# Two fused transformer blocks: all low parts of the weights made by VectorE, none by GpSimd

## The chip, the cores and the metric

The kernel runs on one core of a Trainium2 chip. Five engines work side by side, each through its own instructions in their written order: TensorE (PE in the rows: matmuls and transposes; PEld is its weight load), VectorE (DVE), ScalarE (ACT), GpSimd (POOL) and SyncE (SP), which here starts the loads of the weights. An engine waits at a semaphore when an operand or a buffer is not ready, and all that stands behind that instruction in its queue waits too. The metric is device time in microseconds of one execution, lower is better; several runs give a median.

## The reference

Two blocks follow each other on 256 tokens of width 1024, all in fp32.

```python
# first block: layer 0 MoBA, layer 1 forgetting attention (FoX), both 16 heads of 64
for layer in range(2):
    hn = rms_norm(h, attn_norm[layer])
    ...
    h = h + merge_heads(mix) @ w_o[layer]
    h = h + squared_relu_mlp(rms_norm(h, mlp_norm[layer]), w_up[layer], w_down[layer])
return rms_norm(h, final_norm)

# second block: modulated by c through w_ada
h = modulate(rmsnorm(x, norm_ffn1), sh1, sc1)
x = x + 0.5 * g1 * swiglu(h, ffn1_w_gate, ffn1_w_up, ffn1_w_down)
h = modulate(rmsnorm(x, norm_mix), sh2, sc2)
x = x + g2 * hybrid_mixer(h, ...)          # SSD scan and MLA attention side by side
h = modulate(rmsnorm(x, norm_ffn2), sh3, sc3)
x = x + 0.5 * g3 * swiglu(h, ffn2_w_gate, ffn2_w_up, ffn2_w_down)
return rmsnorm(x, norm_final)
```

## The kernel before

The weights (240 MB) pass through the core once, as slabs of 128 partitions by 1024 fp32 numbers. SyncE loads a slab into `raw` (5 buffers). To keep fp32 precision each slab is split in two: a rounded high part `wh`, a cast by ScalarE (L174), and a low part `wl` = raw - wh, a subtraction with two inputs in SBUF (L175). Both go into tiles with 5 buffers. A product is then three matmuls: high by high, high by low, low by high (L212 to L214 where tokens are the rows of the result, L245 to L247 where features are). The activations are split in the same way by `split`: cast L259 on ScalarE, subtraction L260 on VectorE. Slabs that carry a gain take the lines L178 and L179 instead and always have both halves on ScalarE and VectorE.

The low part at L175 is VectorE's work, except for 38 slabs which the set `on_pool` names: these are GpSimd's. Some first slabs of a stage are made early, before their stage begins (the `early` argument): in pieces, with the cast L167 to `qh` and the subtraction L168 to `ql`. All 18 of these `ql` are GpSimd's.

What stands where in each queue is decided by the program's order. `take(i)` hands a slab to the matmuls and prepares up to two slabs ahead of it; side jobs such as the softmax of the attention are generators which `tick()` advances by a step after each piece of matmuls. So the instructions for a future slab come to stand between instructions of the softmax, on each engine in the same relative order. TensorE's order is fixed as well: pieces of a projection, then a piece of attention, then a projection again.

The stages are named A0 (MoBA layer), M0 (its MLP), A1 (FoX layer), M1, F1 (first SwiGLU), the mixer, F2 (second SwiGLU). In A0 and A1 the attention of 8 heads goes in six halves through `half`: VectorE makes the biased scores `pr` (L620 in A0, L627 in A1) and their maximum `m` (L532); ScalarE the exponentials with their sum (L535); VectorE the reciprocal `rs` (L539), GpSimd the product of pr and rs (L540); TensorE transposes it (L545), ScalarE copies the transposed `pT` out (L547), TensorE multiplies by the values (L638), and the result is split (L259, L260). On ScalarE a slab's wh L174 often stands right behind the exponentials and the pT of an earlier half behind that.

Where one stage hands over to the next, the residual is finished and normalised before TensorE can begin: into F1 by `two_norms_chain` (VectorE's L844, L1020, L1024 on four pieces, ScalarE's square sums, GpSimd's `v` L310, L1028 and `y` L317, then VectorE's `hn` L980 and TensorE's transposes L265); into the mixer and F2 by `norm_chain` with VectorE's `gated` L988, `h` L989, `hn` L1000 in their place. In the mixer, `log1p_of` (L335 to L344, small operations on VectorE) leads to `dA` (L1148), with which TensorE goes on at L1152.

Of the kernel before, what the change touches and what calls it, by code (L numbers as in the profile page):

```python
# [13 lines left out]
OP = mybir.AluOpType  # L14
# [8 lines left out]
F2 = 2816  # L23
# [5 lines left out]
def kernel(ctx: ExitStack, tc: tile.TileContext, a: dict, out: bass.AP):  # L29
    nc = tc.nc  # L30
    PE, ACT, DVE, POOL = nc.tensor, nc.scalar, nc.vector, nc.gpsimd
# [34 lines left out]
    def tt(shape, name="t", dt=F32):  # L66
        return tiny.tile(list(shape), dt, tag="t", name=name)

    def f(ap):
        return ap.bitcast(F32)  # L70
# [43 lines left out]
    ada_order = [(None, j, half, kk) for j in range(9) for half in range(2) for kk in range(4)]  # L114
    mixed = {"rate": 0.0, "due": 0.0}
    hold = []
    on_pool = set()

    def slab(w, r0, nk, c0, n, gain=None, m=None, early=0):


        m = m or max(1, 1024 // n)
        got = []
        for k in range(0, nk, m):
            j = min(m, nk - k)
            plan.append((w, r0 + k * TP, j, c0, n, None if gain is None else gain[k:k + j], len(got) < early))
            got.append(len(plan) - 1)
            mixed["due"] += mixed["rate"]
            if mixed["due"] >= 1 and ada_order:
                mixed["due"] -= 1  # L130
                plan.append(ada_order.pop(0))
        return got
# [22 lines left out]
    def prepare():  # L155
        i = at["prep"]
        raw, e = ready.pop(i), plan[i]
        at["prep"] += 1
        if e[0] is None:
            ada_step(raw, *e[1:])  # L160
            return
        m, n, gain = e[2], e[4], e[5]
        if e[6]:
            ready[i] = []
            for k in range(m):
                hi, lo = pair("q", (TP, n))
                ACT.copy(hi, raw[:, k])  # L167
                POOL.tensor_tensor(lo, raw[:, k], f(hi), op=OP.subtract)  # L168
                ready[i].append((hi, lo))
            return  # L170
        hi = whp.tile([TP, m, n], F32R, tag="wh", name="wh")
        lo = whp.tile([TP, m, n], F32R, tag="wl", name="wl")
        if gain is None:
            ACT.copy(hi, raw)  # L174
            (POOL if i in on_pool else DVE).tensor_tensor(lo, raw, f(hi), op=OP.subtract)  # L175
        else:
            for k in range(m):
                ACT.mul(hi[:, k], raw[:, k], gain[k])  # L178
                DVE.scalar_tensor_tensor(out=lo[:, k], in0=raw[:, k], scalar=gain[k], in1=f(hi[:, k]),  # L179
                                         op0=OP.mult, op1=OP.subtract)  # L180
        ready[i] = [(hi[:, k], lo[:, k]) for k in range(m)]
        at["live"] += 1

    def take(i):

        load_ahead()
        more = 0 if hold else 2 if i else 1
        while at["prep"] < len(plan):
            e = plan[at["prep"]]
            if at["prep"] > i:  # L190
                early = e[0] is not None and e[6]
                if not more or not (early or at["live"] < WB):
                    break
                more -= e[0] is not None and not early
            prepare()
            load_ahead()
        return ready[i]
# [56 lines left out]
    def pair(tag, shape=(TP, 512)):  # L254
        return sb(tag, shape, F32R, tag + "h"), sb(tag, shape, F32R, tag + "l")
# [133 lines left out]
    def plan_attention(qkv, w_o):  # L389
        ids = {}  # L390
        for g in range(2):
            for n in ((2, 0, 1) if g == 0 else (0, 1, 2)):
                w, c0, gain = qkv[n]
                ids["qkv"[n], g] = slab(w, 0, 8, c0 + g * 512, 512, gain)
        for g in range(2):
            for s in range(2):
                ids["o", g, s] = slab(w_o, g * 512, 4, s * 512, 512)
        return ids

    def plan_hidden(ups, w_down, cuts, rate, early=0, after=0):  # L400

        up, down = [], []
        for j in range(len(cuts) + 1):
            mixed["rate"] = rate if after < j < len(cuts) - 1 else 0.0
            if j < len(cuts):
                c0, n = cuts[j]
                up.append([slab(w, 0, 8, c0, n, g, m=2 if n == 512 else 4, early=early if j + i == 0 else 0)
                           for i, (w, g) in enumerate(ups)])
            if j > 0:
                c0, n = cuts[j - 1]  # L410
                down.append([slab(w_down, c0, n // TP, s * 512, 512) for s in range(2)])
        mixed.update(rate=0.0, due=0.0)
        return up, down
# [5 lines left out]
    A0 = plan_attention([(wq, n * D, g_attn[0]) for n in range(3)], a["w_o"][0])  # L419
    M0 = plan_hidden([(a["w_up"][0], g_mlp[0])], a["w_down"][0], MLP_CUTS, 0.5, after=1)  # L420
    A1 = plan_attention([(a["fox_w_q"][0], 0, g_attn[1]), (a["w_kv"], 0, g_kv), (a["w_kv"], D, g_kv)], a["w_o"][1])
    M1 = plan_hidden([(a["w_up"][1], g_mlp[1])], a["w_down"][1], MLP_CUTS, 0.45)
    F1 = plan_hidden([(a["ffn1_w_gate_2"][0], None), (a["ffn1_w_up_2"][0], None)], a["ffn1_w_down_2"][0], FFN_CUTS,
                     0.55, 3)
    X = {"dt": slab(w_in, 0, 8, 2560, 400, early=3), "ckv": slab(w_in, 0, 8, 2960, 288, m=2),
         "bc": slab(w_in, 0, 8, D + 1024, 512)}
# [8 lines left out]
    for n, (r0, c) in enumerate(((D, 73), (D + 512, 77), (0, 65), (512, 69))):  # L435
        for s in range(2):
            X["out", n, s] = slab(w_out, r0, 4, s * 512, 512, col_list(cols2, c, 4))
    F2 = plan_hidden([(a["ffn2_w_gate_2"][0], None), (a["ffn2_w_up_2"][0], None)], a["ffn2_w_down_2"][0], FFN_CUTS,
                     0.3, 3)
# [36 lines left out]
    def ada_step(raw, j, half, kk):  # L476
        n = 2 * j + half
        if kk == 0:
            if half == 0:
                ada[j] = dram.tile([1, D], F32, name=f"mod{j}")  # L480
            ada["acc"] = ada.pop("next", None) or ada_begin(n)
        acc = ada["acc"]
        for i in range(2):
            k = 2 * kk + i
            DVE.scalar_tensor_tensor(out=acc, in0=raw[:, i, :], scalar=c_act[:, k:k + 1], in1=acc,  # L485
                                     op0=OP.mult, op1=OP.add)
        if kk == 2 and n < 17:
            ada["next"] = ada_begin(n + 1)
        if kk == 3:
            POOL.partition_all_reduce(acc, acc, TP, ReduceOp.add)  # L490
            row = acc[0:1, :]
            if j in (2, 8):
                POOL.tensor_scalar(row, row, 0.5, None, op0=OP.mult)
            nc.gpsimd.dma_start(ada[j][:, cols(half)], row)
# [956 lines left out]
        token_first([X["out", 3, s] for s in range(2)], last_part, acc, False, update)  # L1451


    for x, picks in ((A0["o", 0, 1], (0, 1)), (A0["o", 1, 1], (0, 1)), (A1["o", 0, 1], (0, 1)),
                     (A1["o", 1, 1], (0, 1)), (F1[0][0][0], (3,)), (X["bc"], (0, 1, 2)), (X["xs", 0], (0,)),
                     (X["xs", 1], (2, 3)), (X["z", 0], (0, 1, 2, 3)), (X["z", 1], (0, 1, 3)), (X["ckv"], (0,)),
                     (A0["o", 0, 0], (0, 1)), (A0["o", 1, 0], (0,)), (A1["o", 0, 0], (1,)), (A1["o", 1, 0], (1,)),
                     (F1[0][1][0], (0, 1)), (F2[0][0][0], (1,)), (F2[0][1][0], (1,)), (M0[1][-1][0], (1,)),
                     (F1[1][-1][0], (0,)), (F1[1][-1][1], (0, 1)), (F1[0][0][1], (0,)), (F2[0][0][1], (0, 3))):
        on_pool.update(x[n] for n in picks)  # L1460


    keep = const
    squares = []
    xT, vs, chains, go = residual_chain(True)
# [51 lines left out]
    ss, z = [tt((TP, 3), "ss") for _ in range(2)], {}  # L1517
# [77 lines left out]
```

## Time and profile before

| | |
|---|---|
| time, median of 3 runs | 1193.81 us (1193.0 to 1198.21) |
| the profiled execution's own time | 1193.64 us |
| its span in the profile | 1191.9 us |
| busy: TensorE, VectorE, ScalarE, GpSimd | 1160.6, 825.5, 673.5, 304.0 us |
| weights and other data moved | 243.04 MB |

The span is what the profile covers of one execution; about 1.7 us lie around it. Busy time is the sum of an engine's instructions, so it does not say which engine the others wait for. The granted clock is the share of TensorE's full speed that the chip allowed in a stretch; 1.00 is the upper level.

### The profile page before, as it was taken

How to read it: one execution, taken by the hardware profiler on the slowest of the kernel's cores; microseconds unless marked ns; L12 is line 12 of the kernel's file. 1: busy time of each engine (PE TensorE's matmuls, PEld its weight loads, DVE VectorE, ACT ScalarE, POOL GpSimd, SP SyncE). 2: the span in 40 equal slices, each digit the busy share in tenths (PEclk: the TensorE clock that was granted, in tenths of full speed). 3: DMA queues.
4: the chain of work that ended last, by engine and by line, in shares of the span. 5: the costliest groups of instructions: out<-in, count | busy, mean ns of one | idle time of the engine just before them, and what ended most of it. 6: DMA issues, size and time to landing. Idle time of an engine off the chain costs nothing.

```text
span 1191.9 us, 19960 instructions
## 1 busy us (share of the span) xinstructions
PE 1160.6 (97%) x7669; PEld 1050.1 (88%) x7669; DVE 825.5 (69%) x1156; ACT 673.5 (57%) x1147; POOL 304.0 (26%) x260
## 2 busy tenths in 40 slices
PE   8999999999999999999989999999999999999997
PEld 7987989988898799999868999979987887999996
DVE  6654678886666477887477778757777667776445
ACT  6576675665556676557545444545766563544443
POOL 3054201222003501121153131154157224112002
PEclk9999999999999999999989999999999999999999
DMA  8643568887544357899638988743732373877660
GB/s 272 198 138 107 177 229 269 297 269 241 163 160 127 121 174 268 273 336 306 212 93 266 313 285 301 268 146 114 218 100 89 106 234 109 274 226 245 203 194 36
DMA packets 128479, 243.04 MB, mean 204 GB/s; under 512 B 8515, under 2 KB 16612, under 8 KB 128384
## 3 DMA queue, kind: packets, MB, share of 16 engines
q1 hardware_dynamic: 126688, 239.96, 61.8%
q0 software_dynamic: 1376, 1.28, 0.5%
q8 instruction: 60, 0.98, 0.3%
q10 hardware_dynamic: 320, 0.53, 0.1%
q14 instruction: 35, 0.29, 0.1%
HBM read 240.65 MB, written 1.09 MB: 203 GB/s over the span
## 4 chain that ended last, share of the span: by engine, by line
PE 84%; DVE 6%; ACT 3%; POOL 2%; issue 2%; DMA 1%; SPq 0%; POOLq 0%; DVEq 0%; ACTq 0%
PE mm L247 11%; PE mm L246 11%; PE mm L245 11%; PE acc L212 11%; PE acc L214 10%; PE acc L213 10%; PE acc L245 3%; PE acc L246 3%; PE acc L247 3%; PE mm L212 2%; PE mm L213 2%; PE mm L214 2%; PE mm L265 1%; POOL wl L175 1%; PE mm L638 1%
## 5 line engine op out<-in xcount | busy, mean ns | idle before, releaser
L174 ACT CAST wh<-raw 128x1024 fp32r<-128x1024 f32 (+1 forms) x231 | 237.5, 1041 | 221.4 <-DMA raw<-in_w_down_dram 55.9
L175 DVE TENSOR_TENSOR wl<-raw,wh 128x1024 fp32r<-128x1024 f32 (+1 forms) x193 | 258.0, 1351 | 140.1 <-ACT wh L174 136.2
L245 PE MATMUL mm<-xh,wh 128*128 128x256 f32 x1088 | 308.5, 284 | 0.0
L247 PE MATMUL mm<-xh,wl 128*128 128x256 f32 x1088 | 307.9, 283 | 0.0
L246 PE MATMUL mm<-xl,wh 128*128 128x256 f32 x1088 | 307.8, 283 | 0.0
L179 DVE SCALAR_TENSOR_TENSOR wl<-raw,cols,wh 128x512 fp32r<-128x512 f32 (+1 forms) x270 | 202.2, 799 | 69.6 <-ACT wh L178 69.6
L178 ACT ACTIVATE wh<-raw,cols 128x512 fp32r<-128x512 f32 (+1 forms) x270 | 176.3, 709 | 68.6 <-PE acc L246 20.1
L246 PEld LDWEIGHTS mm<-xl,wh 128*128 128x128 f32 x1088 | 208.8, 192 | 0.8
L245 PEld LDWEIGHTS mm<-xh,wh 128*128 128x128 f32 x1088 | 208.7, 192 | 0.8
L247 PEld LDWEIGHTS mm<-xh,wl 128*128 128x128 f32 x1088 | 208.7, 192 | 0.0
L212 PE MATMUL acc<-wh,mh 128*128 128x512 f32 x524 | 207.4, 396 | 0.0
L213 PE MATMUL acc<-wl,mh 128*128 128x512 f32 x524 | 205.1, 391 | 0.0
L214 PE MATMUL acc<-wh,ml 128*128 128x512 f32 x524 | 205.0, 391 | 0.0
L490 POOL PARTITION_ALL_REDUCE ada<-ada x18 | 67.0, 3720 | 334.9 <-DVE ada L485 149.9
L175 POOL TENSOR_TENSOR wl<-raw,wh 128x1024 fp32r<-128x1024 f32 (+1 forms) x38 | 91.4, 2408 | 129.3 <-ACT wh L174 124.1
L214 PEld LDWEIGHTS acc<-wh,ml 128*128 128x128 f32 x524 | 98.8, 189 | 21.1
L212 PEld LDWEIGHTS acc<-wh,mh 128*128 128x128 f32 x524 | 98.9, 189 | 20.7 <-issue 1.6
L213 PEld LDWEIGHTS acc<-wl,mh 128*128 128x128 f32 x524 | 99.0, 189 | 18.9
L485 DVE SCALAR_TENSOR_TENSOR ada<-raw,c_act,ada 128x512 f32<-128x512 f32 x144 | 109.6, 761 | 2.7
L245 PE MATMUL acc<-xh,wh 128*128 128x256 f32 x352 | 102.0, 290 | 0.0
L246 PE MATMUL acc<-xl,wh 128*128 128x256 f32 x352 | 99.5, 283 | 0.0
L247 PE MATMUL acc<-xh,wl 128*128 128x256 f32 x352 | 99.5, 283 | 0.0
(318 smaller groups left out, 1631.4 us busy)
## 6 DMA issues: line engine op xcount, KB each, us to landing
raw<-in_w_ada_dram SPq DMA_DIRECT2D x72, 512.0 KB, 5.4
raw<-in_w_up_dram SPq DMA_DIRECT2D x64, 512.0 KB, 4.9
raw<-in_w_down_dram SPq DMA_DIRECT2D x64, 512.0 KB, 5.5
raw<-in_ffn_w_gate_dram SPq DMA_DIRECT2D x44, 512.0 KB, 4.8
raw<-in_ffn_w_up_dram SPq DMA_DIRECT2D x44, 512.0 KB, 4.5
raw<-in_ffn_w_down_dram SPq DMA_DIRECT2D x44, 512.0 KB, 5.1
raw<-in_moba_w_qkv_dram SPq DMA_DIRECT2D x23, 512.0 KB, 4.9
raw<-in_w_in_dram SPq DMA_DIRECT2D x20, 512.0 KB, 4.1
```

The costliest lines, as they stand in the source:

```text
L174: ACT.copy(hi, raw)
L175: (POOL if i in on_pool else DVE).tensor_tensor(lo, raw, f(hi), op=OP.subtract)
L178: ACT.mul(hi[:, k], raw[:, k], gain[k])
L179: DVE.scalar_tensor_tensor(out=lo[:, k], in0=raw[:, k], scalar=gain[k], in1=f(hi[:, k]), op0=OP.mult, op1=OP.subtract)
L212: PE.matmul(p, lhsT=xh, rhs=wh, start=first and n == 0, stop=False)
L213: PE.matmul(p, lhsT=xh, rhs=wl, start=False, stop=False)
L214: PE.matmul(p, lhsT=xl, rhs=wh, start=False, stop=last and n == len(ws) - 1)
L245: PE.matmul(o, lhsT=wh[:, c], rhs=xh, start=k == 0 and n % 2 == 0, stop=False)
L246: PE.matmul(o, lhsT=wh[:, c], rhs=xl, start=False, stop=False)
L247: PE.matmul(o, lhsT=wl[:, c], rhs=xh, start=False, stop=k == 7 and n % 2 == 1)
L485: DVE.scalar_tensor_tensor(out=acc, in0=raw[:, i, :], scalar=c_act[:, k:k + 1], in1=acc, op0=OP.mult, op1=OP.add)
L490: POOL.partition_all_reduce(acc, acc, TP, ReduceOp.add)
```

## The change

The set `on_pool` is deleted. The 38 low parts that it named (37 of 128x1024, one of 128x576) and the 18 early ones (12 of 128x512, 6 of 128x400) are VectorE's. The arithmetic is the same.

```diff
-    on_pool = set()
...
                 hi, lo = pair("q", (TP, n))
                 ACT.copy(hi, raw[:, k])
-                POOL.tensor_tensor(lo, raw[:, k], f(hi), op=OP.subtract)
+                DVE.tensor_tensor(lo, raw[:, k], f(hi), op=OP.subtract)
...
             ACT.copy(hi, raw)
-            (POOL if i in on_pool else DVE).tensor_tensor(lo, raw, f(hi), op=OP.subtract)
+            DVE.tensor_tensor(lo, raw, f(hi), op=OP.subtract)
...
-    for x, picks in ((A0["o", 0, 1], (0, 1)), (A0["o", 1, 1], (0, 1)), (A1["o", 0, 1], (0, 1)),
...
-        on_pool.update(x[n] for n in picks)
```

The orders of TensorE, ScalarE and SyncE are the same before and after. VectorE's has more rows, GpSimd's fewer. Line numbers behind the first deleted line are one lower in the changed kernel. On VectorE in A0, where kT is the scaled key tile and the halves of the softmax follow each other, there stood before:

```order
L708 SCALAR_TENSOR_TENSOR kT<-acc,rrow 128x512 x2
L539 RECIPROCAL rs<-sm 128x2
L620 SCALAR_TENSOR_TENSOR pr<-dist,mm 128x256 x2
L532 TENSOR_REDUCE m<-pr 128x2
L539 RECIPROCAL rs<-sm 128x2
L620 SCALAR_TENSOR_TENSOR pr<-dist,mm 128x256 x2
L532 TENSOR_REDUCE m<-pr 128x2
L620 SCALAR_TENSOR_TENSOR pr<-dist,mm 128x128 x4
L532 TENSOR_REDUCE m<-pr 128x4
L260 TENSOR_TENSOR ml<-mm,mh 128x512
```

and there stands now, with the slabs' low parts between them:

```order
L707 SCALAR_TENSOR_TENSOR kT<-acc,rrow 128x512 x2
L174 TENSOR_TENSOR wl<-raw,wh 128x1024
L538 RECIPROCAL rs<-sm 128x2
L619 SCALAR_TENSOR_TENSOR pr<-dist,mm 128x256 x2
L531 TENSOR_REDUCE m<-pr 128x2
L174 TENSOR_TENSOR wl<-raw,wh 128x1024
L538 RECIPROCAL rs<-sm 128x2
L619 SCALAR_TENSOR_TENSOR pr<-dist,mm 128x256 x2
L531 TENSOR_REDUCE m<-pr 128x2
L174 TENSOR_TENSOR wl<-raw,wh 128x1024
L619 SCALAR_TENSOR_TENSOR pr<-dist,mm 128x128 x4
L531 TENSOR_REDUCE m<-pr 128x4
```

A wl (L174 now) has come to stand ahead of the first rs and behind each of the two maxima m that follow. In A1 the same happens at six places, in A0 at seven.

The second place is VectorE's queue at the hand-over into F1, where the last slabs of M1 are followed by the residual (L844) and the two norms. Before:

```order
L260 TENSOR_TENSOR ml<-sq,mh 128x512 x2
L175 TENSOR_TENSOR wl<-raw,wh 128x1024 x4
L844 SCALAR_TENSOR_TENSOR h_102<-acc,r_5015,h_102 128x512
L1020 TENSOR_TENSOR u<-h_102,fin 128x512
L1024 TENSOR_TENSOR h_102<-u,mod 128x512
L844 SCALAR_TENSOR_TENSOR h_102<-acc,r_5015,h_102 128x512
```

Now:

```order
L259 TENSOR_TENSOR ml<-sq,mh 128x512 x2
L174 TENSOR_TENSOR wl<-raw,wh 128x1024 x4
L167 TENSOR_TENSOR ql<-raw,qh 128x512 x6
L174 TENSOR_TENSOR wl<-raw,wh 128x1024
L843 SCALAR_TENSOR_TENSOR h_102<-acc,r_5015,h_102 128x512
L1019 TENSOR_TENSOR u<-h_102,fin 128x512
L1023 TENSOR_TENSOR h_102<-u,mod 128x512
L843 SCALAR_TENSOR_TENSOR h_102<-acc,r_5015,h_102 128x512
```

The six ql and one wl have come in ahead of the residual. On GpSimd, in the same place, the norm chain's v and y stood behind them:

```order
L168 ISA
L168 TENSOR_TENSOR ql<-raw,qh 128x512 x6
L175 TENSOR_TENSOR wl<-raw,wh 128x1024
L310 TENSOR_SCALAR v<-ss 128x1
L310 TENSOR_SCALAR v<-su 128x1
```

and they now stand first (the ISA row is a change of GpSimd's library, which has moved to the next instruction that needs it):

```order
L493 DMA mod_5792<-ada 16x1x32
L309 ISA
L309 TENSOR_SCALAR v<-ss 128x1
L309 TENSOR_SCALAR v<-su 128x1
L1027 TENSOR_SCALAR v<-v 128x1
L316 TENSOR_TENSOR y<-v,minus_half 128x1 x2
```

Nothing but v and y is left there for GpSimd.

## Rows read from the trace of the kernel before

**Rows 1.** The page: busy time of each engine (share of the span) and instructions.
```profile
PE 1160.6 (97%) x7669; PEld 1050.1 (88%) x7669; DVE 825.5 (69%) x1156; ACT 673.5 (57%) x1147; POOL 304.0 (26%) x260
```

**Rows 2.** Waits by engine, TensorE: total us, times, longest.
```profile
PE mm L265 <- DVE hn L980: 9.9, 4, 4.0
...
PE mm L1152 <- DVE dA L1148: 1.1, 1, 1.1
PE mm L545 <- POOL pr L540: 1.0, 2, 0.6
```

**Rows 3.** Busy us by stretch (instructions), then TensorE clock, DMA share, GB/s.
```profile
core 0: us, PE busy (x) PEld busy (x) DVE busy (x) ACT busy (x) POOL busy (x), PEclk, DMA share, GB/s
80.00:100.00 20.00, 19.38 (x131) 14.77 (x130) 8.88 (x25) 13.64 (x39) 12.93 (x9) 1.00 0.41 126
...
600.00:620.00 20.00, 15.61 (x65) 12.13 (x64) 14.94 (x20) 7.54 (x18) 10.34 (x12) 0.83 0.23 76
...
980.00:1000.00 20.00, 17.31 (x75) 14.01 (x74) 15.18 (x19) 6.28 (x14) 10.26 (x10) 0.91 0.42 131
```

**Rows 4.** Groups by line and shape on GpSimd (POOL): busy, mean ns.
```profile
L175 POOL TENSOR_TENSOR wl<-raw,wh 128x1024 fp32r<-128x1024 f32 x37 | 90.0, 2435 | 124.1 <-ACT wh L174 118.9 <-DVE pr L627 5.0
...
L168 POOL TENSOR_TENSOR ql<-raw,qh 128x512 fp32r<-128x512 f32 x12 | 18.5, 1580 | 55.0 <-ACT qh L167 55.0
```

**Rows 5.** The same view on VectorE (DVE).
```profile
L175 DVE TENSOR_TENSOR wl<-raw,wh 128x1024 fp32r<-128x1024 f32 x189 | 253.7, 1356 | 132.1 <-ACT wh L174 128.1 <-PE mm L247 2.7
```

**Rows 6.** Chain of waits 782 to 812, into the mixer: start us, us, what.
```profile
785.17 2.75 POOL wl L175
...
795.66 1.43 DVE hn L1000
...
800.61 0.67 DVE hn L980
```

**Rows 7.** Chain of waits 592 to 620, into F1.
```profile
596.95 4.72 POOL ql L168 x3
601.67 2.80 POOL wl L175
...
607.72 0.76 DVE hn L980
```

**Rows 8.** Timeline of VectorE, 590 to 610: start us, us, instruction.
```profile
592.11 1.22 DVE L175 TENSOR_TENSOR wl<-raw,wh 128x1024 fp32r<-128x1024 f32 x1 [1.49 <-ACT wh L174]
```

**Rows 9.** Chain of waits 976 to 1000, into F2.
```profile
985.46 1.67 DVE hn L1000
...
990.80 0.76 DVE hn L980
```

**Rows 10.** Chain of waits 818 to 832, up to dA.
```profile
822.79 1.97 DVE z L337
...
825.46 0.20 DVE r L342
825.68 2.41 DVE r L342
```

**Rows 11.** Timeline of VectorE in A0, with [idle before <-releaser].
```profile
75.50 0.69 DVE L532 TENSOR_REDUCE m<-pr 128x2 f32<-128x512 f32 x1
...
80.67 0.69 DVE L532 TENSOR_REDUCE m<-pr 128x4 f32<-128x512 f32 x1
...
92.96 0.69 DVE L532 TENSOR_REDUCE m<-pr 128x2 f32<-128x512 f32 x1
95.83 1.44 DVE L175 TENSOR_TENSOR wl<-raw,wh 128x1024 fp32r<-128x1024 f32 x1 [2.18 <-ACT wh L174]
...
98.02 0.69 DVE L532 TENSOR_REDUCE m<-pr 128x2 f32<-128x512 f32 x1
...
105.87 0.69 DVE L532 TENSOR_REDUCE m<-pr 128x2 f32<-128x512 f32 x1
```

**Rows 12.** Timeline of VectorE in A1: first and last of eight maxima.
```profile
376.98 0.69 DVE L532 TENSOR_REDUCE m<-pr 128x2 f32<-128x512 f32 x1
...
407.20 0.69 DVE L532 TENSOR_REDUCE m<-pr 128x2 f32<-128x512 f32 x1
```

More of the change, by code (lines that the diff above doesn't have):

```diff
@@ L1451, in mixer @@
         token_first([X["out", 3, s] for s in range(2)], last_part, acc, False, update)
-    for x, picks in ((A0["o", 0, 1], (0, 1)), (A0["o", 1, 1], (0, 1)), (A1["o", 0, 1], (0, 1)),
[L1455 to L1459, printed above, removed]
-        on_pool.update(x[n] for n in picks)
     keep = const
```

## The prediction

> **What bounds the kernel now.** I read the page's busy line first. TensorE is busy 1160.6 of 1191.9 us, VectorE 825.5, ScalarE 673.5, GpSimd 304.0 [rows 1]. So the kernel is TensorE's, with 31 us in which it does not work, and anything that happens on VectorE or GpSimd counts only where TensorE comes to wait for it. The second view, the waits by engine, names those places: the largest is TensorE's transposes L265 waiting for VectorE's hn L980, 9.9 us in 4 times with a longest of 4.0 [rows 2]; all else there is under 2 us. The third view, busy time and granted clock by stretch, says how near TensorE is to its limit: 19.38 of 20 us inside the first attention stage, but 15.61 and 17.31 in two stretches where one block hands over to the next (into F1, the first SwiGLU, and into F2, the second), and there the granted clock is 0.83 and 0.91 instead of 1.00 [rows 3]. A third hand-over, into the mixer at 800 to 820, reads like F2's. A mean of 0.83 over 20 us is 6.8 us at the lower of the two levels (1.2 instead of 2.4 GHz), 0.91 is 3.6 us. Each fall follows one of the long L265 waits; shorter waits elsewhere were not followed by one.
>
> The change therefore has two separate questions: what it gives back in the hand-overs, and what it takes in stages where TensorE is now fed just in time. VectorE's mean load says little on either.
>
> **What moves, and its price.** On GpSimd a low part of 128x1024 takes 2.43 us in the mean of 37, a ql of 128x512 1.58 us (12 of them) [rows 4]. VectorE makes the same 128x1024 in 1.36 us, mean of 189 [rows 5]; that mean holds some stretched by what GpSimd does beside them, so I take 1.2 to 1.4. For a ql on VectorE no row exists; the nearest is hn L980, also 128x512 with two SBUF inputs, 0.67 us where nothing disturbs it [rows 6], and I take 0.7. So VectorE gets some 37 x 1.3 + 12 x 0.7 + 6 x 0.6 (128x400, by width) + 0.8 (128x576) = 61 us more, 886 of 1192, and GpSimd loses about 118. Neither total sets the end. GpSimd keeps L540, which normalises the softmax, and the norm chains v, y; they now wait for nothing of this kind.
>
> **Gains: the hand-overs.** In the F1 hand-over the chain of waits runs through GpSimd: three ql 4.72 us, then wl 2.80 from 601.67, then GpSimd's own v and y, and hn L980 on VectorE only at 607.72 [rows 7]. With the change these stand on VectorE behind the slab that it begins at 592.11 and ends at about 593.3 [rows 8]: six ql end at 593.3 + 6 x 0.7 = 597.5, wl at 598.7, and three groups L844, L1020, L1024 (0.7 each, 2.2 with gaps) follow to 605.2. hn then starts some 2.5 us sooner. TensorE's idle shrinks from 4.0 to about 1.5, which I take to keep its clock: of the 6.8 us at half clock about 5 were spent working, 2.5 us lost. F1 gives 5.0 us.
>
> The three groups in F1 also stop being stretched, and that is where the other hand-overs gain. In the mixer's, hn L1000 took 1.43 us, and in F2's 1.67 [rows 6, 9], against about 0.7 for such 128x512 work; in the chain ahead of dA two small operations, z L337 and r L342, took 1.97 and 2.41 us, where their like next to them take 0.2 [rows 10]. All of these have two SBUF inputs and ran while GpSimd worked on a wl or ql. The Trainium skill states this ("SBUF — State Buffer", section Who interferes with whom: a VectorE instruction with two SBUF inputs contends with a GpSimd instruction that reads SBUF); the trace agrees with 2.41 against 0.2. By that rule alone every one of these would go back to its short time and the change would only gain, which is the first rival below.
>
> Mixer hand-over: GpSimd's wl at 785.17 takes 2.75 and frees the buffer into which the next slab is loaded [rows 6]; done on VectorE that load starts about 1.5 us sooner, and the stretched operations shorten. hn L980, now at 800.61, comes about 1.6 sooner; with the 1.7 us of its half-clock stretch, 3.2. F2: the six ql end by the time that they end now, the stretched h and hn shorten, hn L980 moves from 990.80 [rows 9] to about 989.1: 1.7, with the clock 3.4. The dA chain: two operations shorten by 1.8 and 2.2, so the 1.1 us that TensorE waits for dA [rows 2] goes: 1.2. Gains: 5.0 + 3.2 + 3.4 + 1.2 = **12.8 us**. Bounds: only the waits without the clock, 2.5 + 1.6 + 1.7 + 1.2 = 7; all of the 9.9 plus the 1.1 plus clock, 16.
>
> **Losses: the attention stages.** A0 is the MoBA layer, A1 the FoX layer. Their softmax is a ring over three engines. VectorE makes the maximum m L532; ScalarE's exps L535 wait for it; behind the exps in ScalarE's queue stands the cast wh L174 of the next slab, and behind that the copy pT L547 that TensorE's L638 waits for. In the kernel before VectorE is free to go on to the next pr and m as soon as the exps' sums arrive, while GpSimd takes wh and makes wl beside it: from m at 75.50 two such intervals, to m at 80.67, take 5.17 us together [rows 11]. In the change wl stands in VectorE's queue between m and the next rs, pr, m. It waits for a wh that itself waits for exps that wait for the m before: VectorE and ScalarE go in lock-step.
>
> The trace of before holds one such step, because one slab there is VectorE's already. m at 92.96, wl at 95.83 after 2.18 us of waiting for wh, 1.44 us of work, next m at 98.02: 5.06 us [rows 11]. That is my price of a step. Of the seven intervals between the eight maxima in A0, four are shorter now: the two from 75.50 to 80.67, 5.17 us, and the two from 98.02 to 105.87, 7.85 us [rows 11]. All four get a wl. Lifted to 5.06 each, 10.12 a pair, they cost 4.95 + 2.27 = 7.2 us. A fifth wl stands ahead of the first of them and delays m by its 1.2; the two others stand in the long intervals, behind ml L260, and I give them 1.2 together, one duration for the interval that ends at 92.96 and nothing for the other. A0: 9.6 us of lag on a chain which TensorE meets in order. It has little slack there: 0.6 us of idle in 20 [rows 3], and two L545 already wait for pr [rows 2].
>
> A1 is the same loop, eight maxima from 376.98 to 407.20, 30.2 us against 30.4 [rows 11, 12]; six wl move, the one ahead of the first m is VectorE's already. That would be 9.6 - 1.2 = 8.4; two of its intervals look shorter than in A0, so I take 9. Bounds for each layer: nothing, if TensorE's slack hides it, and 12, if all seven intervals gain one wl and its wait.
>
> The mixer's attention and SSD part has ten moved wl, but between them VectorE also runs operations that GpSimd stretches now. I put their net at +2, from 0 to +4. New idles of some 4 us in A0 and A1 may cost a fall of the clock, as the hand-overs show; TensorE would be waiting through most of it: +1.4 for both. The slabs in F1 and F2 behind the hand-overs and the one at the end of M0 lie in stretches where TensorE has work for several us: 0, and if that cover is gone 1.3 each.
>
> **Sum.** 9.6 + 9 + 2 + 1.4 - 12.8 = +9.2 us on the profiled execution's own 1193.64, which is 0.17 under the median of 1193.81: 1202.9, say **1203 us**.
>
> **Rivals.** *Only the gains.* The lock-step exists but ScalarE's wh is done early enough, or TensorE's backlog of matmuls covers a later pT. For it speaks that several L545 use a pr that lay ready for some us; against it, that the pT behind the second exps of a layer has no such reserve. Then 1193.64 - 12.8 + 2 = 1183 us: faster by 0.9%. It decides at the point where L638 waits for pT by less than about 2 us in each layer. The Trainium skill's rule of choice ("GPSIMD Engine Reference", section 4.1, Engine selection) says this side too: elementwise work with two inputs belongs on VectorE, GpSimd being about twice as slow. The trace agrees in the rate, 2.43 against 1.36, and says nothing of the order in the queue.
>
> *They cancel.* The lag is taken up by about half in each layer, 9 us of loss in all with the mixer: 1193.64 + 9 + 2 - 12.8 = 1192. For it: TensorE's order holds matmuls of the projections between the pieces of attention; against: each delay arrives before the next pause.
>
> *Worse.* The hand-overs keep their clock fall, since an idle of 1.5 us is left and other work moves up (gains 7), or the clock falls in both layers while TensorE works: 1193.64 + 9.6 + 9 + 4 + 3 - 7 = 1212.
>
> *It does nothing* can be left out: 56 instructions do change engine.
>
> **How the numbers follow.** Forecast (lock-step, 1198 to 1208) 0.5; worse 0.17; cancel 0.19; only the gains 0.14. A difference under 0.5%, 6 us, can't be told from none here. Slower by that needs over 1199.8, which the forecast's case holds nearly all of: 0.47 + 0.17 = 0.64. Faster needs under 1187.8: 0.14. Same 0.22. The range for 8 in 10 runs from 1189, which leaves out the first rival, to 1213; the likeliest case's own is 1198 to 1208.
>
> **What would show it.** Right: in A0 and A1 TensorE's span of the stage longer by 8 to 11 us, with waits of L638 for pT and of VectorE's wl for wh of about 2 us; steps between maxima of about 5 us where two take 5.17 now; the three dips of the granted clock gone or halved, and L265's waits for hn under 5 us in all; z L337 and r L342 at 0.2; wl on VectorE near 1.2 everywhere. Wrong: steps of m that stay as short as now (then the wh came early), an L265 wait as long as now (then the chain in the hand-over is not GpSimd's), or a new wait of GpSimd for something that I did not move.

## The result, and the profile after

The changed kernel took 1208.74 us (median of 6 runs, 1205.98 to 1209.43), the kernel before 1193.32 us (median of 6, 1191.29 to 1198.21). The ratio is 1.0121, 95% interval 1.0107 to 1.0136: 15 us slower, in the forecast direction and inside the range (1189 to 1213), 6 us more than the forecast 1203 and 0.7 above the 1198 to 1208 of its likeliest case.

The page's busy line answers to [rows 1]. VectorE gained 29 us net and GpSimd lost 119. TensorE gained 10 with the same number of instructions, so some of them took longer:

```profile
PE 1170.6 (97%) x7669; PEld 1057.1 (88%) x7669; DVE 854.5 (71%) x1212; ACT 673.7 (56%) x1147; POOL 184.6 (15%) x204
```

VectorE's busy time rose by less than the 61 us that it was estimated to take over, because what was its own became shorter. The groups of VectorE answer to [rows 5] (columns as there); L174 and L167 are the wl and ql, L341 is the r of the dA chain:

```profile
L174 DVE TENSOR_TENSOR wl<-raw,wh 128x1024 fp32r<-128x1024 f32 x226 | 292.4, 1308 | 150.5 <-ACT wh L173 146.3 <-PE mm L544 2.7
...
L167 DVE TENSOR_TENSOR ql<-raw,qh 128x512 fp32r<-128x512 f32 x12 | 7.4, 684 | 0.0
L167 DVE TENSOR_TENSOR ql<-raw,qh 128x400 fp32r<-128x400 f32 x6 | 3.0, 571 | 0.0
...
L341 DVE SCALAR_TENSOR_TENSOR r<-r,q 128x32 f32<-128x32 f32 x14 | 2.7, 192 | 0.5
```

The ql that had no row before cost 0.68 and 0.57 us, as estimated (0.7 and 0.6).

The waits of TensorE answer to [rows 2]. L264 for hn, 9.9 us before, is 4.1, and the wait for dA is gone; in their place stand waits inside the attention stages:

```profile
PE mm L637 <- ACT pT L546: 6.6, 6, 2.5
PE mm L604 <- DVE ml L259: 4.7, 2, 2.4
PE mm L264 <- DVE hn L979: 4.1, 4, 1.5
PE mm L544 <- POOL pr L539: 2.2, 2, 1.4
```

VectorE's timeline in A0 answers to [rows 11] and shows why:

```profile
79.11 0.69 DVE L531 TENSOR_REDUCE m<-pr 128x2 f32<-128x512 f32 x1
81.95 1.23 DVE L174 TENSOR_TENSOR wl<-raw,wh 128x1024 fp32r<-128x1024 f32 x1 [2.16 <-ACT wh L173]
...
83.94 0.69 DVE L531 TENSOR_REDUCE m<-pr 128x2 f32<-128x512 f32 x1
86.79 1.23 DVE L174 TENSOR_TENSOR wl<-raw,wh 128x1024 fp32r<-128x1024 f32 x1 [2.16 <-ACT wh L173]
...
88.84 0.69 DVE L531 TENSOR_REDUCE m<-pr 128x4 f32<-128x512 f32 x1
...
118.35 0.69 DVE L531 TENSOR_REDUCE m<-pr 128x2 f32<-128x512 f32 x1
```

From m at 79.11 two intervals to m at 88.84 take 9.73 us, where before they took 5.17. In each, VectorE stands idle for 2.16 us in front of a wl, waiting for ScalarE's wh. The last of the eight maxima (at 118.35) lies 39.2 us behind the first, against 30.4.

TensorE's 7669 instructions come in the same order in both traces (but for six matmuls of A1's scores that lie within 1 us of each other), so each start can be set against its counterpart's. The shift grows or shrinks in a few stages only. This table, worked out from those starts, gives what each stage added in us (times of the kernel before; e1 to e8 and b2 are the experiments below, each against the same profile of the kernel before):

| | start, 0-22 | A0, 74-123 | A1, 375-423 | into F1, 591-630 | F1, 630-781 | into mixer, 781-815 | dA, 815-835 | mixer, 846-946 | into F2 and on |
|---|---|---|---|---|---|---|---|---|---|
| changed | +2.5 | +11.0 | +10.9 | -3.0 | 0.0 | -3.1 | -1.3 | +2.6 | -3.8 |
| e1 | -0.4 | 0.0 | 0.0 | -2.9 | +1.1 | -3.1 | -1.3 | +2.6 | -3.8 |
| e2 | -0.4 | +11.5 | +11.2 | -0.8 | 0.0 | -1.5 | 0.0 | 0.0 | -1.6 |
| e3 | +1.3 | 0.0 | 0.0 | -2.8 | +1.4 | -3.1 | -1.3 | +2.6 | -3.8 |
| e4 | -0.4 | +7.4 | +6.6 | -4.3 | +1.7 | -3.1 | -1.3 | +2.6 | -3.8 |
| e5 | +3.1 | 0.0 | 0.0 | -4.3 | +1.2 | -3.1 | -1.3 | 0.0 | -3.8 |
| e7 | +1.4 | +0.1 | 0.0 | -2.4 | 0.0 | -2.9 | -1.3 | 0.0 | -3.3 |
| e8 | +1.7 | 0.0 | 0.0 | -4.3 | +1.5 | -3.1 | -1.3 | 0.0 | -3.8 |
| b2 (before again) | +2.8 | 0.0 | 0.0 | -0.8 | +0.7 | -1.6 | 0.0 | 0.0 | 0.0 |

What TensorE did in the time that the layers added is seen by setting the same work side by side, columns as in [rows 3]. Before, A0 and A1:

```profile
74.00:123.00 49.00, 47.97 (x312) 37.49 (x311) 24.75 (x58) 33.10 (x81) 26.02 (x18) 1.00 0.40 123
375.00:423.00 48.00, 47.18 (x319) 37.11 (x318) 25.63 (x56) 31.08 (x77) 23.38 (x15) 1.00 0.38 121
```

and after:

```profile
76.50:136.50 60.00, 53.76 (x312) 41.09 (x312) 32.45 (x65) 32.78 (x81) 9.92 (x11) 0.91 0.31 102
388.50:447.40 58.90, 51.35 (x318) 40.04 (x318) 32.33 (x62) 30.80 (x77) 9.32 (x9) 0.94 0.31 98
```

TensorE stood idle some 12 us more in the two layers together (5.2 and 6.7), and it was busy some 10 us longer for the same matmuls (5.8 and 4.2), at a granted clock of 0.91 and 0.94 instead of 1.00. So nearly half of the loss shows as matmuls at the lower clock.

The first column of the table is no work of the change: nothing of it stands there. In that execution the first matmuls were 0.43 us apart (these two rows of TensorE's timeline), where before they were 0.23:

```profile
9.40 0.63 PE L212 MATMUL acc<-wl,xh 128*128 128x512 f32 x1
9.83 0.63 PE L213 MATMUL acc<-wh,xl 128*128 128x512 f32 x1
```

The kernel before, run again as b2, shows the same (+2.8), so this column says nothing of the change. The granted clock of the first 20 us reads 1.00 in both profiles; where the longer distance comes from stays open.

The stretches answer to [rows 3]: the second half of A0, and the hand-overs into F1, the mixer and F2, which lie some 20 us later now:

```profile
116.00:136.00 20.00, 17.58 (x100) 13.66 (x99) 10.90 (x20) 11.46 (x26) 2.23 (x3) 0.91 0.27 86
620.00:640.00 20.00, 18.49 (x80) 14.34 (x78) 15.51 (x24) 8.38 (x21) 5.95 (x10) 0.91 0.34 121
820.00:840.00 20.00, 18.31 (x118) 17.28 (x117) 14.54 (x24) 11.96 (x25) 2.50 (x6) 1.00 0.30 101
1000.00:1020.00 20.00, 19.02 (x92) 15.43 (x92) 16.59 (x25) 8.36 (x18) 2.55 (x5) 1.00 0.47 156
```

The clock now falls in the attention stages (0.91 in A0's second half), and in the hand-overs only into F1. It also falls once in the mixer, where before it read 1.00 from 845 to 945:

```profile
910.00:930.00 20.00, 17.64 (x95) 14.44 (x95) 15.41 (x29) 14.16 (x31) 10.04 (x9) 0.91 0.35 105
```

### The profile page after: what moved, and what is told of

Read it like the earlier page. It is cut to its first block, busy times and chain, and to the rows that moved or that the text cites. A ratio compares the mean times of both kernels' runs of the same rounds, so it can differ in the third digit from the quotient of the medians.

```text
span 1207.7 us, 19964 instructions
## 1 busy us (share of the span) xinstructions
PE 1170.6 (97%) x7669; PEld 1057.1 (88%) x7669; DVE 854.5 (71%) x1212; ACT 673.7 (56%) x1147; POOL 184.6 (15%) x204
## 4 chain that ended last, share of the span: by engine, by line
PE 85%; DVE 7%; ACT 5%; issue 2%; POOL 1%; DMA 0%; SPq 0%; POOLq 0%; DVEq 0%; ACTq 0%
PE acc L211 11%; PE acc L213 11%; PE acc L212 11%; PE mm L245 11%; PE mm L246 11%; PE mm L244 11%; PE acc L244 3%; PE acc L245 3%; PE acc L246 3%; PE mm L211 2%; PE mm L213 2%; PE mm L212 2%; ACT pr L534 2%; PE mm L264 2%; ACT wh L173 1%
## 5 line engine op out<-in xcount | busy, mean ns | idle before, releaser
L174 DVE TENSOR_TENSOR wl<-raw,wh 128x1024 fp32r<-128x1024 f32 (+1 forms) x231 | 296.1, 1297 | 150.9 <-ACT wh L173 146.7
L178 DVE SCALAR_TENSOR_TENSOR wl<-raw,cols,wh 128x512 fp32r<-128x512 f32 (+1 forms) x270 | 202.3, 799 | 72.2 <-ACT wh L177 72.0
L534 ACT ACTIVATE pr<-pr,m 128x128 f32<-128x128 f32 (+1 forms) x80 | 35.6, 446 | 73.9 <-DVE m L531 73.9
```

The costliest lines, as they stand in the source:

```text
L174: DVE.tensor_tensor(lo, raw, f(hi), op=OP.subtract)
```

## The experiments

Three theories were tried. **Order**: VectorE's wl costs where it stands between a maximum and the next one and waits for a wh that stands behind the exps. **Load**: VectorE's added work costs wherever it is. And for the gains, **contention and GpSimd's queue** against **chance of the clock**.

**e1, e2: the attention's low parts alone.** e1 is the changed kernel with 13 slabs given back, e2 the kernel before without them in `on_pool`:

```diff
# e1, against the changed kernel
+    on_pool = set()
...
-            DVE.tensor_tensor(lo, raw, f(hi), op=OP.subtract)
+            (POOL if i in on_pool else DVE).tensor_tensor(lo, raw, f(hi), op=OP.subtract)
...
+    for x, picks in ((A0["o", 0, 1], (0, 1)), (A0["o", 1, 1], (0, 1)), (A1["o", 0, 1], (0, 1)),
+                     (A1["o", 1, 1], (0, 1)), (A0["o", 0, 0], (0, 1)), (A0["o", 1, 0], (0,)),
+                     (A1["o", 0, 0], (1,)), (A1["o", 1, 0], (1,))):
+        on_pool.update(x[n] for n in picks)
# e2, against the kernel before
-        on_pool.update(x[n] for n in picks)
+        if x[0] not in [A[k][0] for A in (A0, A1) for k in A if k[0] == "o"]:
+            on_pool.update(x[n] for n in picks)
```

> The changed kernel with the 13 low parts of A0 and A1 given back to GpSimd; the other 25 and the 18 ql stay on VectorE. Lock-step theory: the two layers, which lost 11.0 us each in the traces, get that back, and the hand-overs keep their 11 us of gains: 1208.7 - 22 = 1187 us (1184 to 1190), faster than both kernels. Rival, VectorE's added load is the cost wherever it stands: 13 x 1.2 = 16 of the some 50 us that were added go back, so a third of the loss of 15, about 1204 us.

Measured: 1186.22 us against 1193.53, ratio 0.9943 (0.9928 to 0.9958). Both layers are back at 0.0 in the table.

> The kernel before with only the 13 low parts of A0 and A1 moved to VectorE; GpSimd keeps the others and all ql. Lock-step theory: both layers lose 11 us and nothing is gained: 1193.3 + 22 = 1215 us (1212 to 1218), slower than the full change. Rival, added load: 16 us of VectorE's time at the same price, a third of 15: 1198 us.

Measured: 1213.27 us, ratio 1.0173 (1.0157 to 1.0190), A0 +11.5 and A1 +11.2. Thirteen of the 56 moved instructions are the whole loss and more; the load theory had 1204 and 1198.

**e3: same instructions, same engines, other order.** The subtraction of those 13 slabs is kept back when the slab is prepared and written behind the next maximum, or at the latest before the slab's matmuls; the load into its `raw` buffer is held back as long:

```diff
-        while at["dma"] < min(len(plan), at["prep"] + most):
+        while at["dma"] < min(len(plan), min(pend, default=at["prep"]) + most):
...
-            DVE.tensor_tensor(lo, raw, f(hi), op=OP.subtract)
+            pend[i] = lambda: DVE.tensor_tensor(lo, raw, f(hi), op=OP.subtract)
+            if i not in later:
+                pend.pop(i)()
...
+        if i in pend:
+            low_parts(i)
         return ready[i]
+
+    def low_parts(most=99999):
+        for i in [i for i in sorted(pend) if i <= most]:
+            pend.pop(i)()
+        load_ahead()
...
             DVE.tensor_reduce(out=m, in_=pr, axis=AX.X, op=OP.max, negate=True)
+            low_parts()
```

> The changed kernel with the same instructions on the same engines; only in A0 and A1 the VectorE subtraction of a slab is written behind the next maximum m instead of ahead of the next rs, pr, m, so that it no longer stands between ScalarE's exps and the m that they are followed by. Lock-step theory: the step between two maxima goes from 4.83 us back to about 3, TensorE's waits in both layers nearly vanish: 1208.7 - 20 = 1189 us (1186 to 1194). Rival, added load: VectorE's work is the same, so 1209 us within 0.3%.

Measured: 1186.50 us, ratio 0.9937 (0.9920 to 0.9955); A0 and A1 are 0.0. VectorE's timeline of e3 in A0 (L541 is m, L175 wl):

```profile
76.82 0.69 DVE L541 TENSOR_REDUCE m<-pr 128x2 f32<-128x512 f32 x1
77.42 1.22 DVE L175 TENSOR_TENSOR wl<-raw,wh 128x1024 fp32r<-128x1024 f32 x1
...
79.59 0.69 DVE L541 TENSOR_REDUCE m<-pr 128x2 f32<-128x512 f32 x1
80.20 1.22 DVE L175 TENSOR_TENSOR wl<-raw,wh 128x1024 fp32r<-128x1024 f32 x1
```

The step is 2.77 us and the wl starts without idle time: the wh that it reads was cast behind the exps of the maximum before, and it runs while ScalarE works on the exps of this one. VectorE does as much as in the changed kernel (852.9 us busy in all, against 854.5), so load alone does not cost anything here; the order does. With the waits the falls of the clock in both layers are gone too, so the 21.9 us are the price of both together. No run here has the waits without the falls.

**e4: no wait for ScalarE, more work for VectorE.** The cast of the 13 slabs is VectorE's too:

```diff
-            ACT.copy(hi, raw)
+            if i in on_dve:
+                DVE.tensor_copy(hi, raw)
+            else:
+                ACT.copy(hi, raw)
```

> The changed kernel with the cast wh of the 13 slabs of A0 and A1 on VectorE as well, so that VectorE has still more to do there, but does not wait for ScalarE's wh. Lock-step theory: a step is m 0.7 + cast about 1.1 + wl 1.2 + rs, pr 0.9 = 3.9 us instead of 4.83, and ScalarE's pT comes 1 us sooner: about 4 us a layer come back, 1208.7 - 8 = 1200 us (1195 to 1204). Rival, added load: 13 more operations of about 1.1 us on VectorE, a further loss at the same price of 0.3 us per us, 1213 us.

Measured: 1198.55 us, ratio 1.0051 (1.0036 to 1.0066), A0 +7.4 and A1 +6.6. In its timeline (L175 is the cast here, L178 wl, L535 m) a step is 3.30 us:

```profile
76.93 0.69 DVE L535 TENSOR_REDUCE m<-pr 128x2 f32<-128x512 f32 x1
77.53 0.68 DVE L175 CAST wh<-raw 128x1024 fp32r<-128x1024 f32 x1
78.25 1.23 DVE L178 TENSOR_TENSOR wl<-raw,wh 128x1024 fp32r<-128x1024 f32 x1
...
80.23 0.69 DVE L535 TENSOR_REDUCE m<-pr 128x2 f32<-128x512 f32 x1
```

With 13 operations more on VectorE the kernel is 10 us faster than the changed one. Here the cast took 0.68 us, not the 1.1 expected. The place still costs: without any wait for ScalarE a step is 3.30 us where the two short ones of the kernel before took 5.17 together [rows 11], and the layers stay 14.0 us longer than before.

**e5, e8: the mixer's ten low parts.** e5 is e1 with the slabs `X["xs", 0]` (0), `X["xs", 1]` (2, 3), `X["z", 0]` (all), `X["z", 1]` (0, 1, 3) on GpSimd as well; e8 is e3 with the same ten on GpSimd:

```diff
+                     (X["xs", 0], (0,)), (X["xs", 1], (2, 3)), (X["z", 0], (0, 1, 2, 3)), (X["z", 1], (0, 1, 3))):
```

> The kernel of e1 with the ten low parts of the mixer's attention and SSD part given back to GpSimd as well, so that VectorE has only the hand-overs', the dA chain's and the other stages' low parts and all ql. Order theory: the stage 845 to 945, where the changed kernel lost 2.6 us, gets them back: 1186.2 - 2.6 = 1183.6 us (1182 to 1185.5). Rival, contention: VectorE's operations in that stage are stretched again by GpSimd's reads (cT L1202 2.45 us instead of 0.7), which costs about as much, 1186 us or more.

> The kernel of e3 (low parts of A0 and A1 on VectorE, written behind the next maximum) with the ten low parts of the mixer's attention and SSD part on GpSimd. Order theory: 1186.5 - 2.6 = 1184 us (1182 to 1186), no different from e5. Rival, added load: VectorE has 16 us more than in e5, at 0.3 us per us 5 us slower than it.

Measured: e5 1184.03 us, ratio 0.9921 (0.9907 to 0.9934); e8 1183.28 us, ratio 0.9912 (0.9897 to 0.9927). The mixer's +2.6 is 0.0 in both tables, so those ten cost 2.6 us net, stretched operations included. The fall of the clock in the mixer is gone as well: by TensorE's starts 1.1 of the 2.6 us were idle time and 1.5 longer matmuls. The two kernels can't be told apart. Both beat the kernel before by 9 to 10 us. Writing the mixer's low parts later, as in e3, was not tried, so that order is their cause too is not shown.

**e7, b2: the hand-overs.** e7 is the kernel before with VectorE making only one kind of piece at each place; b2 is the kernel before, unchanged.

```diff
-                POOL.tensor_tensor(lo, raw[:, k], f(hi), op=OP.subtract)
+                (DVE if i in F2[0][0][0] else POOL).tensor_tensor(lo, raw[:, k], f(hi), op=OP.subtract)
...
-                     (A1["o", 1, 1], (0, 1)), (F1[0][0][0], (3,)), (X["bc"], (0, 1, 2)), (X["xs", 0], (0,)),
+                     (A1["o", 1, 1], (0, 1)), (X["xs", 0], (0,)),
...
-                     (F1[1][-1][0], (0,)), (F1[1][-1][1], (0, 1)), (F1[0][0][1], (0,)), (F2[0][0][1], (0, 3))):
+                     (F1[0][0][1], (0,)), (F2[0][0][1], (0, 3))):
```

> The kernel before with VectorE making only: the one wl in front of F1 (its six ql stay on GpSimd), the three wl in front of the mixer (the ql there stay), the three wl beside the dA chain, and F2's six ql. Read by stage in TensorE's starts. If each hand-over's chain runs through the named piece alone: F1 2 us earlier (the wl's 2.8 less what VectorE's own operations then set), mixer 1.5, dA 1.3, F2 2.1, and 0 in all other stages: 1193.5 - 7 = 1186.5, to 1183 where the clock does not fall either. If the ql are what counts in F1 and the mixer: F1 under 0.5, mixer under 0.5, 1190 us.

> The kernel before, unchanged, to see which of its falls of the clock come in every execution. If they belong to the kernel: half clock for 6.8 us in front of F1 and 3.4 us in front of the mixer and F2, as in its profile. If they are chance: other lengths or none, with the same waits of TensorE for hn, and TensorE's starts by stage 0.8, 1.5 and 1.6 us earlier there, as in e2, whose hand-overs are those of the kernel before.

e7 measured 1185.44 us, ratio 0.9928 (0.9911 to 0.9944): seven wl and six ql carry nearly all of the gain. TensorE's waits in e7:

```profile
PE mm L265 <- DVE hn L980: 5.3, 4, 2.4
```

In F1 the idle in front of the transposes falls from 4.0 to 2.4 us with the one wl off GpSimd and to 1.5 with the six ql as well; into the mixer from 2.5 to 1.2 and 1.0; into F2, by the ql alone, from 2.7 to 1.0. Since whole pieces move, e7 does not tell GpSimd's queue from the stretching in F1 and in front of the mixer. In the dA chain VectorE's timeline of e2 (first two rows, GpSimd still at its wl) and of e7 (VectorE makes them) show the stretching by itself, with the chain's own instructions the same:

```profile
842.68 1.95 DVE L337 TENSOR_TENSOR z<-dte,q 128x32 f32<-128x32 f32 x1
...
845.11 3.77 DVE L342 SCALAR_TENSOR_TENSOR r<-r,q 128x32 f32<-128x32 f32 x7
```

```profile
819.46 0.19 DVE L337 TENSOR_TENSOR z<-dte,q 128x32 f32<-128x32 f32 x1
...
820.13 1.58 DVE L342 SCALAR_TENSOR_TENSOR r<-r,q 128x32 f32<-128x32 f32 x7
```

b2 took 1194.75 us. Its waits for hn are again 9.9 us in 4 times with a longest of 4.0, but the clock fell elsewhere (stretches as in [rows 3], the mixer's second):

```profile
600.00:620.00 20.00, 15.99 (x70) 12.96 (x69) 16.46 (x20) 7.00 (x19) 13.13 (x14) 0.91 0.33 103
800.00:820.00 20.00, 16.79 (x102) 15.50 (x102) 14.84 (x24) 9.30 (x23) 5.52 (x8) 1.00 0.27 89
980.00:1000.00 20.00, 17.32 (x74) 13.98 (x73) 14.50 (x20) 7.35 (x16) 11.35 (x10) 0.91 0.44 138
```

Into F1 it is about 3.4 us at half clock instead of 6.8, into the mixer none, into F2 about 3.4 again. In e2, with the same three waits, the clock reads 0.91, 1.00 and 1.00 there. The waits belong to the kernel; whether a fall follows one of 2.5 or 2.7 us, and how long the one behind 4.0 us lasts, differs from one execution to the next.

## Why the prediction came out as it did

**The lock-step** held in mechanism and price. Predicted was a step of 5.06 us where wl waits for wh; measured are 4.83 and 4.90 with 2.16 us of idle in each. The lag of A0's last maximum against the kernel before, less the 2.5 of the start, is 118.35 - 105.87 - 2.47 = 10.0 us, predicted 9.6. By terms: the first pair of intervals cost 4.6 (predicted 4.95), the second 2.3 (2.27), the wl ahead of the first 1.1 (1.2), and the fifth interval, a lock-step before already, became 0.2 shorter. The two long intervals cost 2.3 instead of 1.2; TensorE's matmuls in them ran partly at half clock (from 92.6 to 99.4), which the term did not hold. e3 shows that it is the order: with the same instructions on the same engines in another order, both layers cost 0.0. The first rival, that only the gains would count, failed at its deciding point: L637 waits for pT, 6.6 us in 6 times, 2.9 of them in A0 and 3.8 in A1, where it wanted less than about 2 in each.

**Its size** was taken a little too small. The layers cost 21.9 us in the trace; the sum had 9.6 + 9 + 1.4 = 20.0. A1, which I took over from A0 without its own intervals, cost as much as A0 (10.9), and the clock fell twice in each layer, not once. The reason given for the small +1.4, that TensorE would be waiting through most of a fall, does not hold: its matmuls were busy 10 us longer for the same work. The sum comes near all the same because it priced A0 by the lag of VectorE's maxima (10.0 measured), and TensorE's 11.0 stayed close to that lag, though half of them were slow matmuls; that is partly luck. How much of the 21.9 us would be left without the falls stays open.

**The waits in the hand-overs** came out to a tenth: hn for L265, 9.9 less 2.5 + 1.6 + 1.7, predicted 4.1, measured 4.1; the dA chain 1.3, predicted 1.2. e7 confirms the pieces one by one. The step inside F1 was wrong in what is late next. I had VectorE's three groups set the start of hn. In the trace of after, the chain goes from the wl through the first group and the first operation of the second to ScalarE's square sum and GpSimd's v and y, which are no shorter than before:

```profile
621.28 1.22 DVE wl L174
...
625.38 0.73 ACT junk L297 x2
...
628.40 1.14 POOL y L316
...
629.56 0.76 DVE hn L979
```

That both give 2.5 us is luck.

**The clock in the hand-overs** is the term that failed. I counted 2.5 + 1.7 + 1.7 = 5.9 us as given back, from one execution. By the table the three hand-overs gave 3.0 + 3.1 + 3.8 = 9.9 against that profile, 5.8 of them waits, so 4.1 of clock; against b2, which had fewer falls, 2.2 + 1.5 + 3.8 = 7.5, so 1.7. And the idle of 1.5 us in F1 "which I take to keep its clock" was followed by a fall in the changed kernel, in e1 and in e3, and by none in e4, e5 and e8.

**The mixer** cost 2.6, predicted 2. The prediction had no fall of the clock there; the changed kernel has one.

**The rest** of the 6 us is the start: +2.5 in this profile, 0 in that of the kernel before. 20.0 + 2 - 12.8 = 9.2 was predicted; 21.9 + 2.6 - 11.2 + 2.5 = 15.8 stands in the traces, and 15.4 between the medians. How the start went in the executions that were not profiled is not known, so how much of the 15.4 is the start stays open.

**Small slips in the sums.** For the mixer's hand-over 1.6 + 1.7 is 3.3, not 3.2. The rival "They cancel" says that its 9 us hold the mixer and then adds the mixer's 2 once more; 1192 is right for 9 us in the two layers alone. Neither moves the forecast by more than 0.1 us. One sign was missed: wl on VectorE is not near 1.2 us everywhere, its mean is 1.31 (1.36 before).

**Two rules that the prediction weighed.** The contention rule (Trainium skill, "SBUF — State Buffer", section Who interferes with whom) agrees with 1.95 against 0.19 us for z L337. The rule that two-input elementwise work belongs on VectorE (Trainium skill, "GPSIMD Engine Reference", section 4.1, Engine selection) agrees in the rate, 2.43 us against 1.22 to 1.36. Read as a rule for the whole kernel it would have had e2 faster; e2 is 1.7% slower, because the rule speaks of an operation's time and not of what stands behind it in the queue.

What stays open: the 0.7 to 1.7 us which some executions lose inside F1, around 756, where TensorE waits for a wl. b2 has some of it, the changed kernel, e2 and e7 none; no run here tells why.

## What to carry to other kernels

Before moving work to a faster engine, write down what stands behind it in that engine's queue and what it waits for: an operation that waits for engine B, put between two operations that B waits for, joins both engines into one chain, and then the faster operation costs more than the slow one did beside it. Here the cure was not the other engine but a place a few rows later in the same queue (e3). In a hand-over, where one chain runs and nothing else is left, the faster engine gave back what stood on that chain and no more: into F1 1.6 us for one wl, 0.9 for six ql. Where GpSimd's work beside it stopped, VectorE's operations there stopped being stretched (the dA chain).

## What was not expected of the hardware

The same program at the same waits has its clock fall or not: half clock for about 6.8, 3.4 and 3.4 us in the three hand-overs in one execution of the kernel before, 3.4, none and 3.4 in another. These two also differ by 2.8 us in the first 22 us. An estimate of what the clock gives back should come from several profiles. VectorE's cast of 128x1024 to the rounded type took 0.68 us, its subtraction of the same size 1.22, ScalarE's cast 1.04.
